# A second MLP whose residual is turned by DVE and ScalarE, with its norm's factor in the split inputs

## The chip, the cores and the metric

The kernel runs on one core of a Trainium2 chip. The metric is the device time of one execution in microseconds, as the median over several runs. Five engines work beside each other, each through its own queue in order: PE (matrix products, TensorE), DVE (VectorE), ACT (ScalarE), POOL (GpSimd) and SP (SyncE, which issues most DMAs). PEld is PE's loading of weights, which overlaps PE.

## The reference

A decoder trunk of two layers over 512 tokens of 1024 channels, in float32. Layer 0 mixes tokens by causal pooling, layer 1 by sliding-window attention; each mixer is followed by a gated MLP with a causal convolution of width 3 over the tokens. The change lies in the MLP of layer 1 and in the norm ahead of it:

```python
def rms_norm(x, g):
    xf = x.astype(jnp.float32)
    y = xf * lax.rsqrt(jnp.mean(xf * xf, axis=-1, keepdims=True) + RMS_EPS)
    return (y * g.astype(jnp.float32)).astype(x.dtype)

def conv_glu_ffn(h, w_in, conv_w, conv_b, w_out):
    u = h @ w_in
    c = lax.conv_general_dilated(
        u, conv_w[:, None, :].astype(u.dtype), window_strides=(1,),
        padding=[(CONV_W - 1, 0)], dimension_numbers=('NWC', 'WIO', 'NWC'),
        feature_group_count=2 * D_FF) + conv_b
    a, g = c[..., :D_FF], c[..., D_FF:]
    return (a * jax.nn.silu(g)) @ w_out
...
        hn = rms_norm(h, norm_ffn[i])
        h = h + conv_glu_ffn(hn, ffn_w_in[i], ffn_conv_w[i], ffn_conv_b[i], ffn_w_out[i])
    return rms_norm(h, norm_f)
```

D_FF is 2816. The factor of the norm, one number for each token, is the same for all channels of that token, so it may be applied to the inputs of the product with `w_in` or to its outputs.

## The kernel before

The residual `h` lies transposed: eight tiles `h[0]` to `h[7]` of 128 channels x 512 tokens, two to a buffer (`hp[0]` to `hp[3]`). Products are made from three passes: both operands are split into a high half (`_h`, rounded for PE) and a low half (`_l`, the rest), and `mm3` (L87) adds high x high (L89), high weight x low input (L90) and low weight x high input (L91). ScalarE makes the high half of a weight (L103) and DVE the low one (L106); `fetch` (L95) is SP's DMA. There are three buffers for raw weights and four for each half.

The attention stage ends with the output projection (L1229 to L1234). For each of eight `m` it adds PE's result to `h[m]` (DVE, L1232), splits `h[m]` times the norm's gain into `f1x{m}_h` (ScalarE, L243) and `f1x{m}_l` (DVE, L244), and gives the square (ScalarE, L211) to `norm2.add`, which adds it up on POOL (L220). These split inputs have the gain in them, but not the factor of the token.

The MLP of layer 1 (`mlp`, L770) runs `mlp_in` (L689). It has 44 chunks, (j, 1) and (j, 0) for j = 0 to 21: the gate and the value half of 128 columns. Chunks 0 to 3 are one group, with four PSUM banks side by side: for each of eight k, PE makes the three passes for all four. From chunk 4 on a group is one chunk, and six banks take turns. After the first group the program names the norm's sum (`norm.stats`, L222: a reduction on DVE at L225, a PE product over partitions at L226, and three Newton steps on DVE), after the second its spreading over the tokens (`norm.spread`, L231: ScalarE L234, DVE transpose L236), and then the convolutions of the chunks done so far.

`conv_chunk` (L678) multiplies the bank by the token factor `rb` into the SBUF tile `u` (L681), makes the first tap on ScalarE (L684) and adds the others on DVE (L685, L686). The gate half goes through Silu (L724), the two are multiplied (L733), and the products are summed and split (`split_sum`, L754) for the token stage. After each group `next(turns)` makes one step of `turned` (L785): four PE transposes of the residual (L792) into a bank and a ScalarE copy (L793) into `ht`, which has the tokens on its partitions; eight steps in all. `mlp_tokens` (L796) then adds the second product of the MLP to `ht`, in three sections, the first after chunk 17. It fetches its weights (L810, L811, L817) into the buffers of `hp` as those become free.

What runs when is set by a list scheduler at compile time: each engine's queue takes, of what is ready by the scheduler's own reckoning, what stands earliest in the source. `pin` (`keep_in_program_order`) chains an instruction behind the one traced before it on its engine; `issue_after(x)` queues the instructions of a block that are on `x`'s engine behind `x`. Neither makes an engine wait for anything by itself.

## Time and profile before

| | |
|---|---|
| median of 3 runs | 898.57 us (898.31 to 899.18) |
| the profiled execution | 897.72 us, of which span 895.9 us |
| second MLP's first matmul | 535.0 us after the span's start |
| granted TensorE clock, mean | 0.996 |
| DVE, ScalarE, POOL busy | 78%, 53%, 28% of the span |

The busy times in 40 equal slices of the span (22.4 us each), in tenths, with the clock that PE was granted:

```profile
PE   9999999999999999999999999999999999999996
PEld 8888889999999998898888888888888888888885
DVE  7899998878787876665887472999977888967744
ACT  7756655555464643546887451754534443434434
POOL 4867332313122300427665030001230002300004
PEclk9999999999999999999999999999999999999998
```

Times inside the execution are counted from the span's start. Where rows of the trace overlap (a matmul of 0.39 us starts 0.23 us after the one before), the distance between starts is what the engine needs for one, and the duration is what passes from its start to its result.

### The profile page before, as it was taken

Reading aid. Unit: us, or ns where it says so; the run is one execution under the profiler, and the core shown is the slowest. Engines: PE = TensorE matmul, PEld = TensorE weight load, DVE = VectorE, ACT = ScalarE, POOL = GpSimd, SP = SyncE. Lnnn points to the kernel's source line nnn. Section 1 sums busy time; section 2 is a strip of 40 time slices with the busy share of each in tenths; the row PEclk is TensorE's granted clock in tenths of the full one; section 3 lists DMA queues with packets and bytes.
Section 4 is the critical chain, followed back from the end, with each engine's and each line's share of the span. In section 5 each row is a group of like instructions: output and inputs, shape, how many; then the busy total and the mean of one; then the engine's idle time right before and its main releaser. Section 6 shows DMA issues by size and latency. Waiting matters only on the chain.

```text
span 895.9 us, 12904 instructions
## 1 busy us (share of the span) xinstructions
PE 884.4 (99%) x4770; PEld 765.6 (85%) x4770; DVE 698.0 (78%) x1110; ACT 475.6 (53%) x776; POOL 247.6 (28%) x327
## 2 busy tenths in 40 slices
PE   9999999999999999999999999999999999999996
PEld 8888889999999998898888888888888888888885
DVE  7899998878787876665887472999977888967744
ACT  7756655555464643546887451754534443434434
POOL 4867332313122300427665030001230002300004
PEclk9999999999999999999999999999999999999998
DMA  9444255565656443122110041175384231452202
GB/s 332 140 131 131 93 162 151 150 186 141 165 142 162 122 129 83 60 94 94 48 48 25 24 159 54 71 235 140 72 243 156 96 98 42 94 188 94 94 24 94
DMA packets 37118, 106.82 MB, mean 119 GB/s; under 512 B 3904, under 2 KB 5952, under 8 KB 37056
## 3 DMA queue, kind: packets, MB, share of 16 engines
q1 hardware_dynamic: 33600, 93.69, 31.8%
q0 software_dynamic: 3312, 12.06, 7.8%
q8 instruction: 37, 0.61, 0.3%
q10 hardware_dynamic: 144, 0.26, 0.1%
q14 instruction: 25, 0.20, 0.1%
HBM read 103.90 MB, written 2.10 MB: 118 GB/s over the span
## 4 chain that ended last, share of the span: by engine, by line
PE 89%; DVE 8%; ACT 1%; issue 1%; POOL 0%; ACTq 0%; DVEq 0%
PE bank L89 28%; PE bank L90 28%; PE bank L91 28%; PE bank L1157 1%; PE bank L1185 1%; DVE bank L393 1%; PE bank L288 1%; DVE tl L412 1%; DVE uw_hold_l L468 1%; PE bank L255 1%; DVE a_t L374 1%; ACT sc L1173 0%; DVE a_t L359 0%; DVE ty L420 0%; DVE g_t L358 0%
## 5 line engine op out<-in xcount | busy, mean ns | idle before, releaser
L89 PE MATMUL bank<-f1x_h,wi_h 128*128 128x512 f32 x352 | 137.7, 391 | 0.0
L90 PE MATMUL bank<-f1x_l,wi_h 128*128 128x512 f32 x352 | 137.0, 389 | 0.0
L91 PE MATMUL bank<-f1x_h,wi_l 128*128 128x512 f32 x352 | 136.8, 390 | 0.0
L103 ACT ACTIVATE wi_h<-wi_raw 128x1024 fp32r<-128x1024 f32 x58 | 61.3, 1060 | 86.5 <-PE bank L90 67.3
L91 PEld LDWEIGHTS bank<-f1x_h,wi_l 128*128 128x128 f32 x352 | 66.1, 188 | 13.9
L89 PEld LDWEIGHTS bank<-f1x_h,wi_h 128*128 128x128 f32 x352 | 66.1, 188 | 13.5
L90 PEld LDWEIGHTS bank<-f1x_l,wi_h 128*128 128x128 f32 x352 | 66.1, 188 | 13.5
L106 DVE TENSOR_TENSOR wi_l<-wi_raw,wi_h 128x1024 fp32r<-128x1024 f32 x44 | 53.8, 1225 | 27.0 <-ACT wi_h L103 27.0
L485 POOL TENSOR_TENSOR uw_r_raw<-uw_r_raw,uw_u_raw 128x512 f32<-128x512 f32 x15 | 25.0, 1668 | 161.7 <-DVE uw_hold_l L468 149.0
L106 POOL TENSOR_TENSOR wi_l<-wi_raw,wi_h 128x256 fp32r<-128x256 f32 x56 | 54.0, 994 | 27.3 <-ACT wi_h L103 27.3
L91 PE MATMUL bank<-th,uw_hold_l 128*128 128x256 f32 x180 | 50.9, 283 | 0.0
L90 PE MATMUL bank<-tl,uw_hold_h 128*128 128x256 f32 x180 | 50.9, 283 | 0.0
L89 PE MATMUL bank<-th,uw_hold_h 128*128 128x256 f32 x180 | 50.8, 282 | 0.0
L681 DVE TENSOR_TENSOR c_u<-bank,n_rb 128x512 f32<-128x512 f32 x44 | 30.1, 688 | 22.2 <-PE bank L91 22.0
L220 POOL TENSOR_TENSOR n_acc<-n_acc,n_sq 128x512 f32<-128x512 f32 x14 | 20.4, 1457 | 90.8 <-ACT n_sq L211 90.7
L90 PE MATMUL bank<-f0x_l,wi_h 128*128 128x512 f32 x112 | 43.6, 389 | 0.0
L91 PE MATMUL bank<-f0x_h,wi_l 128*128 128x512 f32 x112 | 43.6, 389 | 0.0
L89 PE MATMUL bank<-f0x_h,wi_h 128*128 128x512 f32 x112 | 43.0, 390 | 0.0
L531 DVE TENSOR_TENSOR h<-bank,h 128x512 f32<-128x512 f32 x48 | 32.9, 686 | 11.8 <-PE bank L91 11.4
L467 ACT ACTIVATE uw_hold_h<-wo_raw 128x512 fp32r<-128x512 f32 (+1 forms) x48 | 28.4, 591 | 25.7 <-PE bank L90 18.8
L686 DVE SCALAR_TENSOR_TENSOR c_t<-c_u,vec,c_t 128x510 f32<-128x510 f32 x44 | 40.9, 932 | 1.2
L823 POOL TENSOR_TENSOR wt_a_raw<-wt_a_raw,wt_s_raw 128x1024 f32<-128x1024 f32 x4 | 11.3, 2835 | 102.5 <-DVE wt_a_l L106 102.5
(437 smaller groups left out, 2771.6 us busy)
## 6 DMA issues: line engine op xcount, KB each, us to landing
wi_raw<-w_in SPq DMA_DIRECT2D x58, 512.0 KB, 3.3
wo_raw<-w_down SPq DMA_DIRECT2D x32, 256.0 KB, 2.7
uw_u_raw<-w_half SPq DMA_DIRECT2D x15, 512.0 KB, 5.5
uw_u_raw<-w_half POOLq DMA_DIRECT2D x15, 512.0 KB, 5.6
uw_r_raw<-w_half SPq DMA_DIRECT2D x15, 512.0 KB, 3.5
wt_a_raw<-w_tok SPq DMA_DIRECT2D x12, 512.0 KB, 3.8
kq_raw<-w_kq SPq DMA_DIRECT2D x10, 512.0 KB, 3.3
wo_raw<-w_o SPq DMA_DIRECT2D x8, 512.0 KB, 3.3
```

The source lines that it names most:

```text
L89: T.matmul(ps, lhsT=wh, rhs=xh, start=start, stop=False, **kw)
L90: T.matmul(ps, lhsT=wh, rhs=xl, start=False, stop=False, **kw)
L91: T.matmul(ps, lhsT=wl, rhs=xh, start=False, stop=stop, **kw)
L103: pin(A.activation(h[:, :n], raw[:, :n], AF.Copy))
L106: (eng or V).tensor_tensor(l[:, o], raw[:, o], h[:, o].bitcast(F32), ALU.subtract)
L220: eng.tensor_tensor(self.acc[:, lo:hi], self.acc[:, lo:hi], sq[:, lo:hi], ALU.add)
L467: A.activation(w[0], raw, AF.Copy)
L485: G.tensor_tensor(r[:, :n], r[:, :n], u[:, n:], ALU.add)
L531: V.tensor_tensor(h[m], ps, h[m], ALU.add)
L681: V.tensor_tensor(u, ps, rb, ALU.mult)
L686: V.scalar_tensor_tensor(t[:, 2:], u[:, : S - 2], cw[0], t[:, 2:], ALU.mult, ALU.add)
L823: G.tensor_tensor(r[:, :n], r[:, :n], raws["s1", s][:, :n], ALU.add)
```

## The change

The convolution no longer multiplies by the factor for chunks 4 to 43. For chunks 0 to 3 it does, now in place in the bank, and the taps of all chunks read the bank instead of the tile `u`, which is gone. The norm's sum is named inside the first group, before its third k, with ScalarE's square root in place of two of the Newton steps; the square root's table is loaded behind the fifth square of the attention stage, and the eighth square is added by DVE instead of POOL. Once the factor is there, the eight pairs `xs[k]` are made anew: `h[k]` times gain and factor (DVE), a high half by ScalarE and a low half by DVE, each written over the pair that the first group has read. The weights of chunk 4 are named between the fourth and the fifth of these, counted from 0, and those of chunks 5 and 6 behind the last. The convolutions of the first group queue behind all this.

`turned` makes four steps of a DVE transpose of `hp[e]` in blocks of 32 x 32, each followed by sixteen ScalarE copies that put a 32-partition piece (256 elements per partition) in its place in `ht`: 64 in all, 16 of them named in the first group, the rest as three behind each later convolution and one behind each Silu. The PE transposes are gone.

```diff
--- before.py
+++ after.py
@@ -95,6 +95,8 @@
         nc.sync.dma_start(raw[:, :n], src)
         return raw
 
+    lows = []
+
     def weights(src, n, name, eng=None, raw=None, step=1024, pin=lambda ins: ins):
 
         raw = raw or fetch(src, n, name)
@@ -103,7 +105,7 @@
         pin(A.activation(h[:, :n], raw[:, :n], AF.Copy))
         for a in range(0, n, step):
             o = slice(a, min(a + step, n))
-            (eng or V).tensor_tensor(l[:, o], raw[:, o], h[:, o].bitcast(F32), ALU.subtract)
+            lows.append((eng or V).tensor_tensor(l[:, o], raw[:, o], h[:, o].bitcast(F32), ALU.subtract))
         return h, l
 
     def part(w, k, m=P):
@@ -118,7 +120,7 @@
 
     def load_root(x, name):
 
-        A.activation(small(sm, 1, 32, tag="root", name=name), x, AF.Sqrt)
+        return A.activation(small(sm, 1, 32, tag="root", name=name), x, AF.Sqrt)
 
     load_root(eps, "root0")
 
@@ -208,7 +210,7 @@
 
         def square(self, c, lo, hi, sq=None):
             sq = sq or sm.tile([P, S], F32, tag="sq", name=f"{self.name}_sq{c}_{lo}")
-            A.activation(sq[:, lo:hi], h[c][:, lo:hi], AF.Square)
+            self.last = A.activation(sq[:, lo:hi], h[c][:, lo:hi], AF.Square)
             return sq
 
         def add(self, c, lo=0, hi=S, eng=G):
@@ -231,7 +233,7 @@
         def spread(self, r):
 
             wide = sm.tile([P, S], F32, tag="sq", name=f"{self.name}_wide")
-            A.activation(wide.rearrange("p (b i) -> p b i", i=SQ), r.unsqueeze(2).to_broadcast([P, NB, SQ]), AF.Copy)
+            self.wide = A.activation(wide.rearrange("p (b i) -> p b i", i=SQ), r.unsqueeze(2).to_broadcast([P, NB, SQ]), AF.Copy)
             rb = sm.tile([P, S], F32, tag="rb", name=f"{self.name}_rb", bufs=1)
             V.transpose(rb, wide)
             return rb
@@ -675,53 +677,79 @@
         for x in fills:
             pass
 
+    taps = []
+
     def conv_chunk(fp, layer, ps, rb, m, name):
 
-        u = fp.tile([P, S], F32, tag="u", name=f"{name}_u", bufs=3)
-        V.tensor_tensor(u, ps, rb, ALU.mult)
+        if rb is not None:
+            V.tensor_tensor(ps, ps, rb, ALU.mult)
         cw = [col(V_CW + (layer * 3 + t) * 2 * NF + m) for t in range(3)]
         t = fp.tile([P, S], F32, tag="t", name=f"{name}_t", bufs=4)
-        A.activation(t, u, AF.Identity, bias=col(V_CB + layer * 2 * NF + m), scale=cw[2])
-        V.scalar_tensor_tensor(t[:, 1:], u[:, : S - 1], cw[1], t[:, 1:], ALU.mult, ALU.add)
-        V.scalar_tensor_tensor(t[:, 2:], u[:, : S - 2], cw[0], t[:, 2:], ALU.mult, ALU.add)
+        taps.append(A.activation(t, ps, AF.Identity, bias=col(V_CB + layer * 2 * NF + m), scale=cw[2]))
+        V.scalar_tensor_tensor(t[:, 1:], ps[:, : S - 1], cw[1], t[:, 1:], ALU.mult, ALU.add)
+        taps.append(V.scalar_tensor_tensor(t[:, 2:], ps[:, : S - 2], cw[0], t[:, 2:], ALU.mult, ALU.add))
         return t
 
-    def mlp_in(fp, layer, xs, norm, ws0, z, turns):
+    def mlp_in(fp, layer, xs, norm, z, turns):
 
         pairs = [k for n, k in GROUPS for _ in range(n)]
         todo = [(j, s) for j in range(NF) for s in (1, 0)]
-        together = 4 if ws0 is None else 2
-        groups = [todo[i : i + together] for i in range(0, 4, together)] + [[t] for t in todo[4:]]
-        conv, pend, r, rb, y = [None, None], [], None, None, None
-        def load(group):
-            return [ws0.pop(0) if ws0 else in_weights(layer, j, s) for j, s in group]
+        groups = [todo[:4]] + [[t] for t in todo[4:]]
+        conv = [None, None]
+
+        def load(group, *more):
+            return [in_weights(layer, j, s, None, None, *more) for j, s in group]
+
+        def turn(n, *behind):
+            with ExitStack() as order:
+                for x in behind:
+                    order.enter_context(tc.issue_after(x.ins))
+                for x in range(n):
+                    next(turns, None)
+
+        def rescale(k):
+            y = fp.tile([P, S], F32, tag="t", name=f"xs{layer}_{k}", bufs=4)
+            V.scalar_tensor_tensor(y, h[k], col(V_NFF + layer * NC + k), rb, ALU.mult, ALU.mult)
+            return pin(A.activation(xs[k][0], y, AF.Copy)), V.tensor_tensor(xs[k][1], y, xs[k][0].bitcast(F32), ALU.subtract)
 
         stops, first = set(), 0
         for n, sums in GROUPS:
             first += 2 * n
             stops.add(min(first - 1 + sums, NF - 1))
-        ahead = load(groups[0])
+        ahead = [load(groups[0])]
         for i, group in enumerate(groups):
-            ws, ahead = ahead or load(group), None
+            ws = ahead.pop(0) if ahead else load(group)
             pss = [bank("ps") for j, s in group]
             for k in range(NC):
+                if i == 0 and k == 2:
+                    r = norm.stats(bank("aux"), root=True)
+                    turn(12, norm.last)
+                    rb = norm.spread(r)
+                    turn(4, norm.wide)
                 for w, ps in zip(ws, pss):
                     mm3(ps, part(w, k), xs[k], k == 0, k == NC - 1)
-            pend += zip(group, pss)
+            if i == 0:
+                for k in range(NC):
+                    if k == 5:
+                        ahead.append(load(groups[1], pin))
+                    behind = rescale(k)
+                for x in (2, 3):
+                    ahead.append(load(groups[x]))
+                    behind += (lows[-1],)
             j, s = group[-1]
-            if s == 1 or j not in stops:
-                ahead = load(groups[i + 1])
-            if rb is None:
-                if len(pend) < 4:
-                    continue
-                if r is None:
-                    r = norm.stats(bank("aux"))
-                    continue
-                rb = norm.spread(r)
-            for (j, s), ps in pend:
-                conv[s] = conv_chunk(fp, layer, ps, rb, s * NF + j, f"c{layer}_{j}_{s}")
+            if i and not ahead and (s == 1 or j not in stops):
+                ahead.append(load(groups[i + 1]))
+            for n, ((j, s), ps) in enumerate(zip(group, pss)):
+                with ExitStack() as order:
+                    for x in () if i else behind[: 3 + n // 2]:
+                        order.enter_context(tc.issue_after(x.ins))
+                    conv[s] = conv_chunk(fp, layer, ps, None if i else rb, s * NF + j, f"c{layer}_{j}_{s}")
+                if i:
+                    turn(3, *taps[-2:])
                 if s == 1:
-                    A.activation(conv[1], conv[1], AF.Silu)
+                    silu = A.activation(conv[1], conv[1], AF.Silu)
+                    if i:
+                        turn(1, silu, taps[-1])
                     continue
                 e, odd = divmod(j, 2)
                 if not odd:
@@ -746,10 +774,7 @@
                         split_sum(y, z[e], 2, 1, 6)
                 else:
                     split_sum(y, z[e], 2 * odd, 2 * odd, 2)
-                if s == 0:
-                    yield j
-            pend = []
-            next(turns, None)
+                yield j
 
     def split_sum(y, z, i, o, n, sign=1.0):
         src = y[:, i : i + n, :].rearrange("p a b -> p (a b)")
@@ -770,13 +795,16 @@
     def mlp(fp, xs, norm):
 
         z, ht = [], []
-        up = mlp_in(fp, 1, xs, norm, None, z, turned(fp, ht))
+        turns = turned(fp, ht)
+        up = mlp_in(fp, 1, xs, norm, z, turns)
         done, first = 0, 0
         for g, (n, sums) in enumerate(GROUPS):
             upto = first + 2 * n
             while done < min(upto + sums, NF):
                 done = next(up) + 1
             zg = z[first // 2 : upto // 2]
+            for x in turns:
+                pass
             if sums:
                 mlp_tokens(g, zg, ht)
             first = upto
@@ -784,14 +812,22 @@
 
     def turned(fp, ht):
 
-        for j in range(NT):
-            ht.append(fp.tile([P, D], F32, tag="ht", name=f"ht{j}", bufs=NT))
-            for a in range(2):
-                ps = bank("aux")
-                for c in range(4):
-                    T.transpose(ps[:, c * P : (c + 1) * P], h[4 * a + c][:, j * P : (j + 1) * P], ident)
-                A.activation(ht[j][:, a * S : (a + 1) * S], ps, AF.Copy)
-                yield
+        whole = fp.tile([P, NT, NC, P], F32, name="ht", bufs=1)
+        ht.extend(whole[:, j].rearrange("p c i -> p (c i)") for j in range(NT))
+        G4 = P // SQ
+        for e in range(NC // 2):
+            x = fp.tile([P, 2 * S], F32, tag="turn", name=f"turn{e}", bufs=1)
+            V.transpose(x, hp[e])
+            x = x.rearrange("p (c j q i) -> p c j q i", c=2, j=NT, q=G4)
+            for g in range(G4):
+                for q in range(G4):
+                    src, dst = slice(g * SQ, (g + 1) * SQ), slice(q * SQ, (q + 1) * SQ)
+                    A.activation(
+                        whole[dst, :, 2 * e : 2 * e + 2, src].rearrange("p j c i -> p c j i"),
+                        x[src, :, :, q, :],
+                        AF.Copy,
+                    )
+                    yield
 
     def mlp_tokens(g, z, ht):
 
@@ -1231,7 +1267,9 @@
                 pass
             V.tensor_tensor(h[m], wo_ps[m], h[m], ALU.add)
             xs2.append(split_scaled(h[m], col(V_NFF + NC + m), f"f1x{m}"))
-            norm2.add(m)
+            norm2.add(m, eng=V if m == NC - 1 else G)
+            if m == NC // 2:
+                pin(load_root(eps, "root2"))
 
 
     with tc.tile_pool(name="fp1", bufs=2) as fp:
```

## The prediction

> **What bounds the kernel now.** I began with the page's busy times and its chain that ended last, for the whole span.
>
> ```profile
> span 895.9 us, 12904 instructions
> ...
> PE 884.4 (99%) x4770; PEld 765.6 (85%) x4770; DVE 698.0 (78%) x1110; ACT 475.6 (53%) x776; POOL 247.6 (28%) x327
> ...
> PE 89%; DVE 8%; ACT 1%; issue 1%; POOL 0%; ACTq 0%; DVEq 0%
> ```
>
> PE is busy for 99% of the span and carries 89% of the chain. The next view is the chain for 530 to 620 us, where the second MLP starts and every edited line runs.
>
> ```profile
> by line: PE bank L91 32.2%; PE bank L90 32.1%; PE bank L89 31.9%; PE bank L792 3.9%; PE bank L226 0.1%
> ...
> 568.52 0.44 PE bank L792 x4
> ...
> 569.43 0.24 PE bank L91
> ```
>
> The whole stretch is PE: matmuls on L89 to L91, a trace of L226 (the norm's sum), and L792 at 3.9%: four transposes of the residual in one row of 0.44 us. The timeline of PE shows whether there is air between the matmuls.
>
> ```profile
> 535.00 0.39 PE L89 MATMUL bank<-f1x_h,wi_h 128*128 128x512 f32 x1
> ...
> 556.76 0.29 PE L226 MATMUL bank<-n_part,groups 128*128 128x16 f32 x2
> 556.90 0.48 PE L89 MATMUL bank<-f1x_h,wi_h 128*128 128x512 f32 x1
> ```
>
> From the first row to L226 the first group's 96 matmuls start in 21.76 us, 0.2267 us each, and the next group follows 0.14 us later: PE has no idle time. A chunk of eight k-steps with three matmuls each is 24 x 0.2267 = 5.44 us. So only two things change the time here: fewer PE instructions, or a new wait of PE.
>
> **The change, part by part.** The transposes go from PE.
>
> ```profile
> L792 PE MATMUL bank<-ident,h x32: 270/272/273, 562.4 to 604.2; 128*128 128x128 f32 x32
> ...
> L793 ACT ACTIVATE ht<-bank x8: 577/581/599, 563.5 to 604.8; 128x512 f32<-128x512 f32 x8
> ```
>
> There are 32, in eight blocks of four. The chain prices a block at 0.44 us: 8 x 0.44 = 3.5 us, and 3.9% of 90 us gives the same. A few matmuls behind each block take 0.24 us (569.43) for 0.23, so 0.3 us more over eight blocks is the most I grant: 3.8. I take 3.5. It lies wholly on the path. With the transposes go eight ScalarE copies of 0.58 us, 4.7 us, which no one waited for.
>
> What replaces them: four block transposes on DVE of 128x1024, each bounded by one and two times L236's 0.71 us below, and 64 ScalarE copies of 256 elements on 32 partitions. These and all later costs lie beside PE; they cost time only where PE gets an operand late. How much room there is:
>
> ```profile
> 537.00:555.00 18.00, 18.00 (x81) 14.85 (x81) 1.67 (x3) 0.48 (x2) 1.79 (x1) 1.00 0.14 48
> 557.00:606.00 49.00, 49.00 (x233) 40.48 (x233) 47.34 (x76) 31.85 (x43) 0.90 (x1) 1.00 0.49 153
> ```
>
> From 537 to 555 us DVE and ScalarE hardly work (1.7 and 0.5 us busy), while PE does the first group. From 557 to 606 us DVE is full (47.3 of 49 us) and ScalarE is not (31.9).
>
> **The norm, moved ahead.** Its sum (L226) stood at 556.8 us; it now stands before k-step 2 of the first group, at 535.0 + 24 x 0.2267 = 540.4 us. Its two PE instructions are moved, not removed. Are its inputs there? The last square ends at 537.2 us, and now DVE adds it instead of POOL:
>
> ```profile
> 536.55 0.62 ACT L211 ACTIVATE n_sq<-h 128x512 f32<-128x512 f32 x1
> ...
> 539.13 0.71 DVE L225 TRANSPOSE_TENSOR_REDUCE n_part<-n_acc 128x16 f32<-128x512 f32 x1 [1.18 <-POOL n_acc L220]
> ```
>
> DVE had idled 1.18 us before the reduction (L225), so it is free at 538.0; one add like L681 (0.69) and the reduction (0.71) end at about 539.4, a microsecond before PE asks. If a block transpose (up to 1.4 us) slips in ahead, PE waits 0.4 us; I cost it at 0 and keep 0.4. From the sum to the spread factor I take layer 0, which uses the square root already:
>
> ```profile
> L226 PE MATMUL bank<-n_part,groups x6: 177/220/263, 44.2 to 556.8; 128*128 128x16 f32 x6
> ...
> L236 DVE STREAM_TRANSPOSE n_rb<-n_wide x3: 705/711/711, 47.9 to 562.6; 128x512 f32<-128x512 f32 x3
> ```
>
> First sum 44.2, end of its transpose 47.9 + 0.7 = 48.6: 4.4 us, with other work among it. So the factor stands at about 545 us, against 563.3 before. One more ScalarE table load, for the root, stands behind the fifth square, near 524 us:
>
> ```profile
> 529.53 1.06 ACT L103 ACTIVATE wi_h<-wi_raw 128x1024 fp32r<-128x1024 f32 x1 [3.24 <-PE bank L90]
> ...
> 554.69 2.96 ACT L103 ACTIVATE wi_h<-wi_raw 128x1024 fp32r<-128x1024 f32 x3 [17.52 <-PE bank L90]
> ...
> 567.29 1.28 ACT L724 ACT_TABLE_LOAD   x1 [0.99 <-DVE c_t L686]
> ```
>
> It takes 1.28 us, and ScalarE idled 3.24 us before 529.53 with only PE's buffer to wait for: nothing. (The load at 567.29, for Silu, stays.)
>
> **The inputs, split anew.** The durations:
>
> ```profile
> L685 DVE SCALAR_TENSOR_TENSOR c_t<-c_u,vec,c_t x44: 742/745/752, 565.1 to 856.8; 128x511 f32<-128x511 f32 x44
> ...
> L106 DVE TENSOR_TENSOR wi_l<-wi_raw,wi_h 128x1024 fp32r<-128x1024 f32 x26 | 31.8, 1226 | 21.6 <-ACT wi_h L103 21.6
> L681 DVE TENSOR_TENSOR c_u<-bank,n_rb 128x512 f32<-128x512 f32 x22 | 14.9, 687 | 5.3 <-PE bank L91 5.1
> L759 DVE TENSOR_TENSOR zl<-y,zh 128x1536 fp32r<-128x1536 f32 x5 | 8.8, 1756 | 0.2 <-ACT zh L757 0.2
> L761 DVE SCALAR_TENSOR_TENSOR zl<-y,zh 128x256 fp32r<-128x256 f32 x5 | 2.1, 420 | 0.5 <-ACT zh L757 0.5
> ...
> L684 ACT ACTIVATE c_t<-c_u,vec 128x512 f32<-128x512 f32 x22 | 17.5, 806 | 1.5 <-DVE c_u L681 1.3
> L757 ACT ACTIVATE zh<-y 128x256 fp32r<-128x256 f32 x5 | 2.0, 409 | 3.9 <-DVE y L733 3.9
> L234 ACT ACTIVATE n_wide<-n_r 128x512 f32<-128x512 f32 x1 | 0.6, 631 | 0.2 <-DVE n_r L200 0.2
> ```
>
> Eight times a product (0.75, like L685), a ScalarE copy (at most 0.63) and a difference (0.69): 8 x 1.44 = 11.5 us of DVE, from 545 to 556.5, inside its idle stretch. Each pair is written in place, so pair 7 waits for the first group's last read at 557.0. ScalarE's copies 1 to 7 are chained to the one before, and 5 to 7 stand behind chunk 4's high half, which waits for PE's buffer (554.69, 1.06 us): free from 555.8, so not in the way. Pair 7 comes at 557.0 + 0.63 + 0.69 = 558.3, and with one weight split (1.23) queued ahead of it at 559.6. PE wants pair 7 after 21 more matmuls, at 556.9 + 4.8 = 561.7. Two microseconds are left: cost 0.
>
> **The convolutions.** Forty chunks lose L681 (0.69), the first four keep it. The taps now read PSUM. L685 above reads SBUF; layer 0's tap reads PSUM:
>
> ```profile
> L358 DVE SCALAR_TENSOR_TENSOR g_t<-bank,vec,g_t x22: 732/750/751, 52.9 to 336.7; 128x511 f32<-128x511 f32 x22
> ```
>
> From PSUM 0.750, from SBUF 0.745 us: I take no difference, and 1.4 us less DVE work for each pair of chunks.
>
> The Trainium skill speaks against this part: its page "VectorE: DVE Perf Modes", section "Rules for kernel authors", has a matmul's output copied to SBUF first where several operations use it, and the section "The TRN2 errata" there gives PSUM sources 62 cycles more. As an estimate from that page this would be 0.06 us a tap, 0.8 us over the twelve taps ahead of chunk 7 below, and rival A would be that much dearer. The two rows do not bear it out.
>
> **Weights of three chunks named ahead.** What PE needs next are the low halves of chunk 7 and 8 (chunks counted from 0). Before:
>
> ```profile
> 555.78 2.36 DVE L106 TENSOR_TENSOR wi_l<-wi_raw,wi_h 128x1024 fp32r<-128x1024 f32 x2 [15.94 <-ACT wi_h L103]
> ...
> 561.47 1.23 DVE L106 TENSOR_TENSOR wi_l<-wi_raw,wi_h 128x1024 fp32r<-128x1024 f32 x1
> ...
> 582.09 1.22 DVE L106 TENSOR_TENSOR wi_l<-wi_raw,wi_h 128x1024 fp32r<-128x1024 f32 x1
> ...
> 562.52 1.06 ACT L103 ACTIVATE wi_h<-wi_raw 128x1024 fp32r<-128x1024 f32 x1 [0.25 <-DMA wi_raw<-w_in]
> ```
>
> The first row is chunks 4 and 5, chunk 6 follows at 558.15, then 7 and 8. Chunk 8's high half was ready at 563.6 and its low one came 18.5 us later: DVE worked off convolutions that stand earlier in the source. Now chunk 7 is the one named after them. DVE from 555.8 until chunk 7's low half, if it goes strictly by the source: three low halves 3.7, three differences 2.1, four convolutions 4 x (0.69 + 0.75 + 0.75) = 8.8, two gate products 1.4, the pair's sums and splits 0.42 + 0.69 + 0.42 + 0.42 + 1.76 = 3.7, chunks 4 and 5 3.0 and 1.1, one block transpose 1.4: 25.2 us, to 581.0; 26 starts each some 0.09 us before the former's end (562.61 less 561.47 is 1.14, not 1.23) make it 578.7, and the half 579.9. PE reaches chunk 7 at 556.9 + 3 x 5.44 = 573.2. It can do its 16 matmuls on the high half first, to 576.8, and chunk 8's, to 580.5. That PE's order does such things the chain shows:
>
> ```profile
> 580.37 0.44 PE bank L792 x4
> 580.81 0.23 PE bank L89
> ...
> 583.07 0.44 PE bank L792 x4
> 583.50 0.36 PE bank L91
> ```
>
> No L91 between 580.4 and 583.5: while the low half was out, PE did high halves and four blocks of transposes. I take 0, since DVE also meets gaps of the Silu chain; the other end is 579.9 - 576.8 = 3.1 us.
>
> **SP's and POOL's queues.** The token stage's weights are fetched into the residual's four buffers as they come free.
>
> ```profile
> SPq L817 <- PE bank L792: 23.2, 2, 20.5
> ...
> 604.70 0.42 SPq L810 DMA_DIRECT2D wt_s_raw<-w_tok  x1
> ...
> wt_s_raw<-w_tok POOLq DMA_DIRECT2D x8, 512.0 KB, 7.4
> ```
>
> Before, such a fetch stood 20.5 us at the head of SP's queue for the transposes, and the last buffers came free with the last block. Now a buffer is free with its block transpose: the first by 545 us, the fourth at the 33rd step after the first group's 16, seven steps to a pair, so behind chunk 13, which PE ends at 556.9 + 10 x 5.44 = 611.3. Its fetch (604.7 before) goes out near 614, and with about 5 us for SP's part and 7.4 for POOL's adding one it lands by 627. The stage's first matmul comes after chunk 17, at 633. Cost 0, with 6 us in hand; chunk weights queued behind a waiting fetch have three buffers ahead of them.
>
> Sum: -3.5 on PE, +0 elsewhere, ends -3.8 and +3.5 of waits (0.4 + 3.1). The profiled execution took 897.72 us (span 895.9, 1.8 around it) and would take 894.2; the three runs' median is 0.85 above it, so 898.57 - 3.5 = 895.1.
>
> **The rivals.**
> A, the cover is gone (18%): the transposes were what PE did while a low half was late. Then their four blocks come back as a wait, 1.8 us, or chunk 7's 3.1: 896.8 to 898.2. For it: DVE's 47.3 of 49 us. Against: eight L681 (5.5 us) leave that stretch, and the rescaling lies before it.
> B, the rescaled inputs come late (12%), slower: the chain sum, root, spread, eight rescalings is serial and PE cannot pass chunk 4 without it. It decides from a factor later than 561.7 - 11.5 = 550.2 us. Should the sum keep its old place in PE's queue, the factor stands at 563.3 as before, pair 7 at 574.8, and PE waits 13.1: 908.2. A factor at 556 costs 5.8 and gives 900.9. Against: by the rows above the factor stands 5 us before 550.2.
> C, ScalarE becomes the bound (4%), slower: a pair of chunks lasts 10.9 us and takes ScalarE 2 x 1.06 + 2 x 0.81 + 0.63 (Silu, the size of L234) + 1.0 (splits: half of L757's 0.41 and 1.5 x 1.06) = 5.4 plus seven copies, so it decides from 0.79 us a copy; at 1.0 us seven pairs run 1.5 over each, 10.3: 905.4. The bounds, 0.41 (L757) and 0.63 (L234, twice the elements), stay under; I take 0.41. The Trainium skill's section "The TRN2 errata" (same page) warns of this: small pieces each pay a fixed cost, and it advises 512 elements or more. Its formula gives, as an estimate, 0.40 us for 256 elements, and L757's 0.41 agrees.
>
> **How the numbers follow.** Forecast 66%, A 18, B 12, C 4. A third of A still ends over 0.2% (1.8 us, about what a measurement of this kernel can tell) below 898.57: faster 0.66 + 0.06 = 0.72, same 0.12, slower 0.12 + 0.04 = 0.16. The range reaches from the largest saving (894.8) to A's end (898.2), with the 0.6 us by which a run shown lies off the median on both sides: 894.2 to 898.8, leaving out B and C and the far end of the waits.
>
> **What would show it.** Right: no L792, PE without idle from 535 us, the span shorter by 3.5; L226 near 540.4, the factor by 546, pair 7's difference before 561; DVE's busy time down by 10 us or more (40 x 0.69 less 11.5 and 5.6). Wrong: PE waiting for xs's pair or for L106's low half between 557 and 585 us, or starts further apart than 0.2267 us; copies over 0.79 us.

## The result and the profile after

| | before | after |
|---|---|---|
| median of the runs shown with the result | 898.88 us (898.28 to 899.78, 6 runs) | 893.17 us (893.01 to 894.47, 6 runs) |
| profiled execution | 897.72 us, span 895.9 | 893.14 us, span 891.3 |

The ratio is 0.994, interval 0.9927 to 0.9953; a second measurement of the kernel after gave 0.9942 (0.9930 to 0.9955), which is 5.2 us (4.0 to 6.3) of 899.01. The forecast was 3.5 us, to 895.1, with a range down to 894.2. So the sign was right, and the time lies 1 us below the range. The page's first lines and its chain of waits, for the kernel after:

```profile
span 891.3 us, 12896 instructions
...
PE 881.1 (99%) x4738; PEld 763.0 (86%) x4738; DVE 682.6 (77%) x1083; ACT 502.8 (56%) x843; POOL 242.7 (27%) x326
...
PE 88%; DVE 8%; ACT 2%; issue 1%; POOL 0%; ACTq 0%; DVEq 0%
```

PE has 32 instructions and 3.3 us less, and 99% of the span as before. The chain for 535 to 625 us, which held 3.9% of transposes, is now only matmuls:

```profile
by line: PE bank L91 33.5%; PE bank L89 33.4%; PE bank L90 33.3%; PE bank L228 0.1%
```

Does PE wait? All its waits in the whole span (the releasing engine and line, total us, times, longest):

```profile
PE bank L257 <- DVE warm L255: 2.2, 1, 2.2
PE bank L89 <- DVE h L533: 0.7, 1, 0.7
```

The first is at the program's start, the second at 118 us, far ahead of the second MLP; within that MLP there is none. So the new work hides entirely, as forecast. What the MLP saved is read from PE's timeline, between its first matmul and the first of the token stage (columns: start, duration, engine, line, operation, output<-inputs, shapes):

```profile
535.58 0.39 PE L89 MATMUL bank<-f1x_h,wi_h 128*128 128x512 f32 x1
...
541.08 0.29 PE L228 MATMUL bank<-n_part,groups 128*128 128x16 f32 x2
...
633.82 0.39 PE L89 MATMUL bank<-wt_a_h,zh 128*128 128x512 f32 x1
```

```profile
637.02 0.39 PE L89 MATMUL bank<-wt_a_h,zh 128*128 128x512 f32 x1
```

Before, that stretch ran from 535.00 (quoted in the prediction) to 637.02: 102.02 us. After, 633.82 - 535.58 = 98.24. The saving is 3.78 us, the upper end of the 3.5 to 3.8 that the transposes were given. I call this stretch the **MLP part** below. From there to the last matmul both kernels take 250.01 us.

But the spans differ by 4.6 us, and the first stretch even grew by 0.58. The rest is at the very end. ScalarE's timeline for the last microseconds, before and after:

```profile
890.73 2.36 ACTq L941 DMA_DIRECT2D out<-o  x1
```

```profile
887.54 0.37 ACTq L977 DMA_DIRECT2D out<-o  x1
```

The same DMA, issued from the same place in the program, holds ScalarE's queue for 2.36 us before and for 0.37 after. From the last matmul's start to the span's end it is 895.89 - 887.03 = 8.86 us before and 891.31 - 883.83 = 7.48 after: 1.38 us that no step of the prediction had. The DMA view of that window of the kernel before names a companion (queue, kind: packets, MB, share):

```profile
q14 instruction: 1, 0.01, 0.5%
...
out<-o ACTq DMA_DIRECT2D x1, 256.0 KB, 4.0
```

One packet on a queue of the kind "instruction" moves there, and the output lands 4.0 us after its issue. In the kernel after, the corresponding window has no such packet, and the landing takes 2.6 us:

```profile
out<-o ACTq DMA_DIRECT2D x1, 256.0 KB, 2.6
```

3.78 + 1.38 - 0.58 = 4.58, the difference of the spans. The questions for the experiments: is the end's 1.4 us real and what makes it; are the 3.8 us the transposes alone; and what do the other parts of the change do, if PE shows no trace of them? One of the eight executions behind the median of "after, not named ahead" in the table below took 1792.4 us, for no known reason, and the ratio there leaves it out.

### The profile page after: what moved, and what is told of

It reads as the page before. It is cut to its first block, busy times and chain, and to the rows that moved or that the text cites. A ratio compares the mean times of both kernels' runs of the same rounds, so it can differ in the third digit from the quotient of the medians.

```text
span 891.3 us, 12896 instructions
## 1 busy us (share of the span) xinstructions
PE 881.1 (99%) x4738; PEld 763.0 (86%) x4738; DVE 682.6 (77%) x1083; ACT 502.8 (56%) x843; POOL 242.7 (27%) x326
## 3 DMA queue, kind: packets, MB, share of 16 engines
q1 hardware_dynamic: 33600, 93.69, 31.9%
## 4 chain that ended last, share of the span: by engine, by line
PE 88%; DVE 8%; ACT 2%; issue 1%; POOL 0%; ACTq 0%; DVEq 0%
PE bank L89 28%; PE bank L90 28%; PE bank L91 28%; PE bank L1193 1%; PE bank L1221 1%; DVE bank L395 1%; PE bank L290 1%; DVE tl L414 1%; ACT sc L1209 1%; PE bank L257 1%; DVE uw_hold_l L470 1%; DVE a_t L376 1%; DVE a_t L361 0%; DVE g_t L360 0%; DVE ty L422 0%
## 5 line engine op out<-in xcount | busy, mean ns | idle before, releaser
L89 PE MATMUL bank<-f1x_h,wi_h 128*128 128x512 f32 x352 | 137.0, 389 | 0.0
L90 PE MATMUL bank<-f1x_l,wi_h 128*128 128x512 f32 x352 | 136.9, 389 | 0.0
L105 ACT ACTIVATE wi_h<-wi_raw 128x1024 fp32r<-128x1024 f32 x58 | 61.4, 1059 | 59.5 <-PE bank L90 43.8
L90 PEld LDWEIGHTS bank<-f1x_l,wi_h 128*128 128x128 f32 x352 | 66.1, 188 | 13.7
L89 PEld LDWEIGHTS bank<-f1x_h,wi_h 128*128 128x128 f32 x352 | 66.1, 188 | 13.5
L90 PE MATMUL bank<-tl,uw_hold_h 128*128 128x256 f32 x180 | 50.9, 283 | 0.0
L89 PE MATMUL bank<-th,uw_hold_h 128*128 128x256 f32 x180 | 50.8, 282 | 0.0
L90 PE MATMUL bank<-f0x_l,wi_h 128*128 128x512 f32 x112 | 43.6, 389 | 0.0
L89 PE MATMUL bank<-f0x_h,wi_h 128*128 128x512 f32 x112 | 43.0, 390 | 0.0
L847 POOL DMA_DIRECT2D wt_s_raw<-w_tok x8 | 7.0, 870 | 120.1 <-DMA wt_s_raw<-w_tok 72.7
L470 DVE TENSOR_TENSOR uw_hold_l<-wo_raw,uw_hold_h 128x512 fp32r<-128x512 f32 (+1 forms) x48 | 36.7, 764 | 3.2 <-ACT uw_hold_h L469 3.2
L1209 ACT ACTIVATE sc<-sc,neg 128x257 f32<-128x257 f32 (+1 forms) x64 | 30.3, 476 | 10.6 <-DVE neg L1196 10.0
```

The costliest lines, as they stand in the source:

```text
L89: T.matmul(ps, lhsT=wh, rhs=xh, start=start, stop=False, **kw)
L90: T.matmul(ps, lhsT=wh, rhs=xl, start=False, stop=False, **kw)
L105: pin(A.activation(h[:, :n], raw[:, :n], AF.Copy))
L470: V.tensor_tensor(w[1], raw, w[0].bitcast(F32), ALU.subtract)
L1209: A.activation(t, t, AF.Exp, bias=neg[:, i : i + 1], scale=-1.0, accum_out=den[:, i : i + 1])
```

## The experiments

Ten more runs were made, one of them of the kernel after once more. The table has for each the MLP part, the time from the last matmul's start to the span's end (both from its one trace), the median and the ratio to the kernel before, measured beside it. Medians of different rows were not all taken beside the same runs of before, so the ratios compare better.

| kernel | MLP part, us | end, us | median, us | ratio (interval) |
|---|---|---|---|---|
| before | 102.02 | 8.86 | 898.88 | 1 |
| after | 98.24 | 7.48 | 893.17 | 0.994 (0.9927 to 0.9953) |
| after again | 98.27 | 7.47 | 893.30 | 0.9942 (0.9930 to 0.9955) |
| before + 40 copies | 102.07 | 7.48 | 897.94 | 0.9985 (0.9976 to 0.9993) |
| after + 56 copies | 98.28 | 7.49 | 893.93 | 0.9944 (0.9924 to 0.9964) |
| after + 60 copies | 98.24 | 8.90 | 895.28 | 0.9956 (0.9941 to 0.9972) |
| after, PE transposes | 102.06 | 7.48 | 898.17 | 0.9982 (0.9973 to 0.9991) |
| after, late norm | 110.61 | 7.47 | 906.98 | 1.0082 (1.0069 to 1.0096) |
| after, not named ahead | 106.09 | 7.46 | 901.48 | 1.0027 (1.0017 to 1.0038) |
| after, factor behind | 103.85 | 7.48 | 899.97 | 1.0014 (1.0004 to 1.0024) |
| before, turn only | 106.47 | 7.49 | 902.08 | 1.0033 (1.0020 to 1.0045) |
| before, turn held | 108.15 | 7.48 | 903.96 | 1.0059 (1.0044 to 1.0075) |

### The end: before with 40 small copies

```diff
-                if s == 0:
-                    yield j
+                if j == 15:
+                    for x in range(40):
+                        pin(A.activation(small(sm, 1, 32, tag="root", name=f"pad{x}"), eps, AF.Copy))
+                yield j
```

> The kernel before, with 40 extra ScalarE copies of 32 elements on one partition issued at chunk 15's group of the second MLP, where the low halves lead PE by over 10 us; nothing else differs. Theory F: the kernel before loses about 1.4 us at its very end because ScalarE's issue of the last output DMA took 2.36 us in its trace, while one 8 KB packet of instructions was fetched on its queue; the kernel after issues it in 0.37 us because its ScalarE program has other lengths. Moving ScalarE's instruction count by 40 then takes the slow issue away: issue of the last DMA 0.3 to 0.5 us, time from the last matmul to the span's end 8.9 -> 7.5 us, time 1.2 to 2.0 us below the kernel before's (about 0.998 of it). Rival: the long issue comes from something else (the output's data, the chip's memory, chance), or it is part of the change itself: issue still near 2.4 us in this profile, time within 0.5 us of the kernel before (ratio 1.000).

The last DMA's issue on ScalarE's timeline:

```profile
893.03 0.37 ACTq L943 DMA_DIRECT2D out<-o  x1
```

0.37 us, the end 7.48, the median 1.6 us and the ratio's middle 1.3 us (0.6 to 2.2) below the kernel before. Forty instructions that do nothing, the last of them 120 us earlier (772 us), made the kernel before faster. Theory F holds in this direction; the rival (chance, or a part of the change) falls.

### The end: after with 56 and 60 small copies

The same loop in the kernel after, with 56 and with 60.

> The kernel after with 56 extra tiny ScalarE copies at chunk 15's group. Theory F (ScalarE's last DMA issue is long when an 8 KB fetch of instructions on its queue falls beside it; fetches stand 128 instructions apart): the fetch moves toward the last DMA's issue, and in one of the three kernels with 56, 60 and 64 copies it falls on it: issue 2.36 us in place of 0.37 and the time from the last matmul to the end 7.5 -> 8.9 us. With 56: the nearest by the count, likeliest with 60. MLP part unchanged at 98.2. Rival: 7.5 us in all three.

> The kernel after with 60 extra tiny ScalarE copies at chunk 15's group. Theory F: as for 56 copies; by the count of ScalarE's instructions this one puts the boundary of a fetch nearest to the last DMA's issue: issue 2.36 us, last matmul to the end 8.9 us, time about 1.4 us above after's (894.6). Rival: 7.5 us as in after.

The last DMA with 56 copies, and then with 60, with the instruction packet in the last microseconds of the latter:

```profile
888.96 0.37 ACTq L980 DMA_DIRECT2D out<-o  x1
```

```profile
888.54 2.39 ACTq L980 DMA_DIRECT2D out<-o  x1
```

```profile
q14 instruction: 1, 0.01, 0.9%
```

With 56 copies nothing happens; with 60 the slow issue is back (2.39 us), the packet of instructions is back beside it, and the end is 8.90 us. Both kernels have the same MLP part. The ratios (0.9944 and 0.9956, from two and four executions) differ by 1.1 us, within their intervals; the traces show the 1.4 directly. A kernel with 64 copies was not run.

That the packet fetches ScalarE's own instructions can be counted in the traces, where ScalarE's instructions (those of its sequencer included) can be numbered. An 8 KB packet of this kind starts right behind the 1088th in the kernel before and right behind the 1216th, 128 further on, with 60 copies; the output's DMA is the 1088th and the 1216th, and is being issued at that moment. With 40 copies the DMA is the 1127th, and the packet goes behind the 1085th, at 856.6 us, 36 us ahead of the DMA. With 56 the DMA is the 1212th, and the packet comes at 893.2 us, after the span's end. In the kernel after the DMA is the 1157th. (Single records can be missing, so the numbers may be off by one or two.)

So the number of instructions on ScalarE's queue decides whether a fetch of its next instructions falls on its last DMA, and 1.4 us of this change's result is that. It belongs to no edited line, and an edit that changes the number of ScalarE's instructions can win or lose it. What the fetch and the issue share was not taken apart; shown is that they come and go together.

### The transposes: after with PE's transposes put back

```diff
-                    turn(12, norm.last)
...
-                    turn(4, norm.wide)
...
-                    turn(3, *taps[-2:])
+                    next(turns, None)
...
-                    if i:
-                        turn(1, silu, taps[-1])
...
+                    for x in range(56):
+                        pin(A.activation(small(sm, 1, 32, tag="root", name=f"pad{x}"), eps, AF.Copy))
...
+                    T.transpose(ps[:, c * P : (c + 1) * P], h[4 * a + c][:, j * P : (j + 1) * P], ident)
+                A.activation(ht[j][:, a * S : (a + 1) * S], ps, AF.Copy)
```

> The kernel after, with the residual turned by 32 PE transposes and 8 ScalarE copies of 512 elements as before, one block per chunk from chunk 4 on, and 56 tiny ScalarE copies at chunk 15 in place of the missing ones, so that ScalarE's instruction count stays that of after. Theory: the transposes alone are what the MLP part saves, so they come back in full: 3.5 to 3.8 us above after's time (896.7 to 897.0), eight rows of 0.44 us in the chain of waits, no other idle time of PE. Rival (rival A of the prediction): PE had idle time or late low halves that transposes cover, or after wins by its other parts too: then less than 2 us above after's time (under 895.2).

The chain of waits for 535 to 625 us, by line:

```profile
by line: PE bank L89 32.3%; PE bank L90 32.1%; PE bank L91 31.9%; PE bank L819 3.9%; PE bank L228 0.1%
```

The 3.9% are back, and the MLP part is 102.06 us: 3.82 more than after, 0.04 from the kernel before. The ratio's middle is 0.0040 above that of after, 3.6 us. The transposes are the whole of what the MLP part saved, 0.48 us for a block: 0.44 for the four, and the rest from the first matmuls behind each, which start 0.24 us apart.

### Rival B's price: after with the norm's sum behind the first group

```diff
                 if i == 0 and k == 2:
-                    r = norm.stats(bank("aux"), root=True)
                     turn(12, norm.last)
-                    rb = norm.spread(r)
-                    turn(4, norm.wide)
...
             if i == 0:
+                r = norm.stats(bank("aux"), root=True)
+                rb = norm.spread(r)
+                turn(4, norm.wide)
```

> The kernel after with the norm's sum and spread issued behind the first group's matmuls instead of ahead of its third k-step; everything else as in after. This prices rival B of the prediction. Theory: the chain from sum to pair 7's difference is serial and PE cannot pass chunk 4 without it: the sum at about 557 us, the factor at 561 to 563, pair 7 near 573 to 575, and PE idle for 10.8 to 13.1 us between 557 and 575, so 904 to 906.3 us. Rival: PE covers part of it by working k-steps in the order in which the pairs come and by other work: idle under 6 us, time under 899.2.

PE's timeline where it waits (in brackets the idle time ahead of the instruction, and what ended it):

```profile
568.57 0.80 PE L89 MATMUL bank<-f1x_h,wi_h 128*128 128x512 f32 x1 [9.68 <-ACT wi_h L105]
569.16 0.63 PE L90 MATMUL bank<-f1x_l,wi_h 128*128 128x512 f32 x1
```

The MLP part is 12.4 us longer, the theory's 10.8 to 13.1; the rival's cover of 5 us or more is not there. But it is made otherwise than I worked it out: PE stands still for 9.7 us, and then its matmuls start 0.43 us apart, not 0.23, up to 573.1. That second piece is 2.4 us. So PE went on from 568.6 us, at half rate, while the last pairs were still being made, and that the sum comes out near the forecast is in part luck. The profile names a high half (L105) as what came last for the 9.7 us, and ScalarE's timeline shows why:

```profile
566.28 1.29 ACT L713 ACTIVATE f1x_h<-xs 128x512 fp32r<-128x512 f32 x2 [1.84 <-DVE xs L712]
567.48 1.04 ACT L105 ACTIVATE wi_h<-wi_raw 128x1024 fp32r<-128x1024 f32 x1
```

Chunk 4's high half is named between pairs 4 and 5, so it stands behind the copies of the first five pairs, and these wait for DVE. PE waited for the place of chunk 4's weights in that order, not for pair 7.

### The weights ahead: after without naming them

```diff
-                for x in (2, 3):
-                    ahead.append(load(groups[x]))
-                    behind += (lows[-1],)
```

> The kernel after without naming the weights of the third and fourth group (chunks 5 and 6 of the order) ahead of the first group's convolutions; each is named one group ahead, as in the kernel before. Theory: the low halves of chunks 5 to 7 stand behind four or more convolutions on DVE then; by after's trace chunk 5's and 6's halves led PE by 3.3 and 7.0 us and chunk 7's by 3.7, and four convolutions (4 x 2.2 = 8.8 us) ahead of them use that up: PE waits 1.8 to 5.5 us on L91's operand, MLP part 100.0 to 103.7 us against 98.2. Rival: PE goes on with high halves of the next chunk and the naming is worth nothing: 98.2 to 98.6.

PE's timeline:

```profile
569.89 0.39 PE L90 MATMUL bank<-f1x_l,wi_h 128*128 128x512 f32 x1
575.30 0.80 PE L91 MATMUL bank<-f1x_h,wi_l 128*128 128x512 f32 x1 [5.02 <-DVE wi_l L108]
```

The last six matmuls up to 569.89 are L89 and L90 alone, so PE used a high half while its low one was out, but for no more than these six; then it stands for 5.0 us. The wait is within the theory's 1.8 to 5.5, but the MLP part is 7.85 us longer, since the next twelve matmuls run 0.43 us apart (2.6 us in all). Removing three lines costs more than the whole change brings.

### The rescaled inputs: after with the factor on every chunk

```diff
-                for k in range(NC):
-                    if k == 5:
-                        ahead.append(load(groups[1], pin))
-                    behind = rescale(k)
+                ahead.append(load(groups[1], pin))
+                behind = ()
...
-                    for x in () if i else behind[: 3 + n // 2]:
+                    for x in () if i else behind[: 1 + n // 2]:
...
-                    conv[s] = conv_chunk(fp, layer, ps, None if i else rb, s * NF + j, f"c{layer}_{j}_{s}")
+                    conv[s] = conv_chunk(fp, layer, ps, rb, s * NF + j, f"c{layer}_{j}_{s}")
```

> The kernel after without the rescaled inputs: the norm's sum and factor stay early, but every chunk's product is multiplied by the factor in its bank (44 products of 0.69 us on DVE in place of 4), and the eight rescalings (8 x 1.44 us of DVE in its idle stretch) are left out. Theory: DVE's work between 557 and 606 us grows by 8 chunks x 0.69 = 5.5 us and it had 47 of 49 us: with the turn's steps in it, low halves of chunks 8 and 9 (0.8 and 0.4 us ahead of PE in after) come late and PE waits 0.5 to 5 us: MLP part 98.8 to 103.2. Rival: the products hide beside PE as they did before, the rescaling is worth nothing and its saving of DVE work is idle time: 98.2 to 98.6, and the last chunks run no later.

PE's timeline at its wait within the MLP part:

```profile
581.07 0.50 PE L91 MATMUL bank<-f1x_h,wi_l 128*128 128x512 f32 x1 [3.66 <-DVE wi_l L108]
```

3.7 us for one low half, and 5.6 us on the MLP part with the slow matmuls behind it: more than the theory's 5. DVE's timeline has the half late:

```profile
579.80 1.22 DVE L108 TENSOR_TENSOR wi_l<-wi_raw,wi_h 128x1024 fp32r<-128x1024 f32 x1
```

DVE does not pause between 570 us and that row, and each chunk's product takes it 0.69 us. A second wait, of 0.53 us, comes in the token stage (at 652.87), and the stretch from the token stage's first matmul to the last one is 0.8 us longer than in after. The rival (hidden anyway, the last chunks no later) falls.

### The turn alone: before with only the block transposes

```diff
-        u = fp.tile([P, S], F32, tag="u", name=f"{name}_u", bufs=3)
+        u = ps
         V.tensor_tensor(u, ps, rb, ALU.mult)
...
-            next(turns, None)
+            for x in range(5):
+                next(turns, None)
```

with the new function that turns the residual.

> The kernel before with only the turn of the residual by DVE and ScalarE (five steps behind each group); the norm, the scale on each chunk and the weights named one chunk ahead stay as they were (the factor is multiplied in the bank in place, since the separate tile would not fit beside the turned residual). Theory: the other parts of the change pay only for DVE's time; without them the four block transposes (1.24 us each) and the 44 products come on top of DVE's queue where it is full, chunk 7's and 8's low halves come later than PE wants them, and PE waits: 1.8 to 3.1 us of the 3.8 saved are given back in the MLP part, first MLP matmul to first token matmul 100.0 to 101.3 us against 102.0 before and 98.2 after. Rival: the transposes' saving stands by itself, and the moved norm, the rescaled inputs and the weights named ahead are worth nothing: 98.2 to 98.6 us, as after.

It is slower than before, 106.47 us for the MLP part. PE waits four times there, for 0.95, 3.06, 0.58 and 1.08 us. The longest wait, on ScalarE's timeline and on PE's:

```profile
554.21 6.81 ACT L798 ACTIVATE ht<-turn 32x256 f32<-32x256 f32 x16 [1.31 <-DVE turn L793]
561.04 2.95 ACT L103 ACTIVATE wi_h<-wi_raw 128x1024 fp32r<-128x1024 f32 x3
```

```profile
562.15 0.50 PE L89 MATMUL bank<-f1x_h,wi_h 128*128 128x512 f32 x1 [3.06 <-ACT wi_h L103]
```

Three lots of sixteen copies, from 537.94 us on, stood ahead of the next chunks' high halves on ScalarE (the expectation below counts 42 of them, the trace has 48). The direction was the theory's, the mechanism at this place was not: ScalarE's order, not DVE's load. The three short waits the profile does put down to DVE. So a second kernel holds the steps, as the change does:

```diff
+                if layer and i == 0 and k == 2:
+                    turn(16, norm.last)
...
+                if layer:
+                    turn(4, *taps)
```

> The kernel before with only the turn by DVE and ScalarE, and the steps held as in the kernel after: 16 of the 68 behind the norm's last square, where DVE and ScalarE idle, and four behind each chunk's last tap. Without the hold (the run before this one of that kind) ScalarE took 42 of the copies ahead of the high halves of chunks 4 to 6, and PE waited 3.1 us for them. Theory S: that run lost its time to the copies' place in ScalarE's queue; held, the turn by itself saves most of the transposes' 3.8 us: MLP part 98.2 to 99.5 us. Rival D: DVE is the limit there without the rescaled inputs and the weights named ahead; PE waits for low halves all the same, with the clock at half rate behind the wait: MLP part 101 to 106 us, as in the runs that leave out one of those two parts (103.9 and 106.1).

PE's timeline, at the longer of its two waits (the other is 0.95 us):

```profile
595.05 0.79 PE L91 MATMUL bank<-f1x_h,wi_l 128*128 128x512 f32 x1 [6.85 <-DVE wi_l L106]
```

Theory S's number falls: with no copies ahead of the high halves of chunks 4 to 6 the MLP part is 108.15 us, longer still than the 101 to 106 of rival D. One low half comes 6.9 us late. On DVE's timeline it stands (at 593.78) behind a tap that waits for ScalarE:

```profile
593.11 0.75 DVE L687 SCALAR_TENSOR_TENSOR c_t<-bank,vec,c_t 128x511 f32<-128x511 f32 x1 [1.21 <-ACT c_t L686]
```

ScalarE's timeline has eight copies ahead of the first tap that this one waits for:

```profile
588.88 3.40 ACT L809 ACTIVATE ht<-turn 32x256 f32<-32x256 f32 x8
592.30 0.78 ACT L686 ACTIVATE c_t<-bank,vec 128x512 f32<-128x512 f32 x1
```

So the copies' place in ScalarE's queue still mattered, now ahead of the taps, and S's idea is not refuted with its number. How much of the 6.9 us is theirs was not taken apart, and both kernels also multiply in the bank in place, where the kernel before has a tile of its own, for want of room. What they do show is that the turn by itself, in these two orders, loses 4.5 and 6.1 us in the MLP part against the kernel before.

### After again

> The kernel after, unchanged, timed in more rounds. The two differences that the traces show are 3.8 us in the second MLP (the transposes) and 1.4 us in ScalarE's last DMA issue: 5.2 us, so a ratio of 0.9942 and about 893.5 to 894.3 us. The first result's 5.7 us would then hold 0.5 us of the run-to-run spread that lies in the first 112 us of every kernel here. Rival: a third gain of the change is still unnamed and the ratio is 0.9936 or less.

The median is 893.30 us and the ratio 0.9942, the theory's value; 0.9936 lies within the interval too, so a further gain below half a microsecond cannot be excluded. The runs fall at 893.2 to 893.3 and at 894.4 to 894.5, and this trace shows one source of such steps: its second MLP starts at 536.91 us, 1.33 later than in the first trace of the same kernel. Over the traces of all kernels here, which differ little up to that point, the start lies between 535.00 and 537.45. Three places make it, all in the first 120 us. In the chain of waits, the 24 warming matmuls at the start take 4.72 us in the trace of before and 5.41 in this one (5.39 in the first trace of after):

```profile
2.23 4.72 PE bank L255 x24
```

```profile
2.23 5.41 PE bank L257 x24
```

Near 110 us PE waits for ScalarE in some traces and not in others. The first trace of after has no such wait; its timeline in this one:

```profile
111.34 0.39 PE L89 MATMUL bank<-th,uw_u_h 128*128 128x256 f32 x1 [0.59 <-ACT sn L650]
```

And the wait for DVE at 118 to 120 us is 0.66 us in the first trace of after and 0.97 in this one. Between these two traces the last two places make nearly all of the difference. The profiled execution of before had the earliest start of all, 0.85 us below its median as a whole. This spread is what a single pair of profiles adds to any comparison here.

## Where the prediction was right, and the step that failed

**PE's transposes.** Right, and under-sized. The block of 0.44 us was measured as 0.48 with what follows it (3.82 us over eight, in the run that puts them back). I had granted 3.8 and taken 3.5; the rows of 0.24 us behind each block were already evidence for the larger value. That is 0.3 us.

**"+0 elsewhere".** This is the step that failed. The sum let ScalarE's eight copies go and 64 come at no cost because no one waits for them, which is right, and took the rest of the program to be untouched, without a reason given. But a step that adds or removes instructions on ScalarE also shifts the places at which its later instructions are fetched (128 apart in these traces), and in the kernel before one of these sat on the last thing that ScalarE does, its 1088th instruction. Its row was there to be read: 2.36 us for a DMA issue, the landing at 4.0 us, and one packet of kind "instruction" in that window. I had followed the chain in the stretch of the edits and had not looked at the 9 us behind the last matmul. It gave 1.4 us, shown by the padded kernels in both directions.

**The range.** Its low end was the largest saving, 3.8, plus 0.6 us of spread. With the end's 1.4 us the sum is 5.2, and 898.57 - 5.2 = 893.4, below it. The second measurement gives these 5.2 us; the half microsecond more in the first (5.7) is within the spread described above and has no cause shown.

**The norm moved ahead.** L228 stands at 541.08, forecast 540.4 plus the 0.58 by which this trace starts later. Its inputs came later than I said, on DVE's timeline:

```profile
536.39 1.24 DVE L820 STREAM_TRANSPOSE turn<-h 128x1024 f32<-128x1024 f32 x1
...
538.77 1.22 DVE L108 TENSOR_TENSOR wi_l<-wi_raw,wi_h 128x1024 fp32r<-128x1024 f32 x1
539.91 0.71 DVE L227 TRANSPOSE_TENSOR_REDUCE n_part<-n_acc 128x16 f32<-128x512 f32 x1
...
544.88 0.71 DVE L238 STREAM_TRANSPOSE n_rb<-n_wide 128x512 f32<-128x512 f32 x1 [0.76 <-ACT n_wide L236]
...
560.14 0.68 DVE L713 TENSOR_TENSOR f1x_l<-xs,f1x_h 128x512 fp32r<-128x512 f32 x1
```

A block transpose slipped in ahead (the case I had kept 0.4 us for), and a low half besides: the reduction ends at 540.62, not 539.4. That left 0.4 us of margin, and PE lost 0.05. The root then stood behind twelve copies on ScalarE:

```profile
537.72 5.11 ACT L825 ACTIVATE ht<-turn 32x256 f32<-32x256 f32 x12
542.85 0.27 ACT L184 ACTIVATE rs_y<-bank,eps 128x16 f32<-128x16 f32 x1
```

It starts 1.5 us after the sum's end at 541.37. Even so the factor stands at 545.6, against 545 to 546 forecast: luck in part, since the 4.4 us taken over from layer 0 happened to leave room for a wait of 1.5 us that I had not seen.

**The rescaling.** Products 0.75, differences 0.68 as priced; pair 7's difference ends at 560.8, 1.2 us after my later bound of 559.6 (0.58 of it is the later start) and before PE's need (561.7, with the later start 562.3). Cost 0, with 1.5 us left. The late-norm run gives the price if that order is lost, 12.4 us; I had said 13.1 for the old place, all of it a wait for pair 7, and 2.4 of the 12.4 are the clock, not a wait.

**Taps, turn and copies.** The rows that group them, for 530 to 625 us (columns: shapes, count, busy us, mean ns):

```profile
L825 ACT ACTIVATE ht<-turn 32x256 f32<-32x256 f32 x55 | 22.8, 415 | 3.5 <-DVE turn L820 2.8
...
L689 DVE SCALAR_TENSOR_TENSOR c_t<-bank,vec,c_t 128x511 f32<-128x511 f32 x15 | 11.1, 744 | 1.6 <-ACT c_t L688 1.6
```

Taps from the bank take 0.744 us, where SBUF gave 0.746: the Trainium skill's page "VectorE: DVE Perf Modes", section "The TRN2 errata", with its 62 cycles more for PSUM is not borne out by this kernel for a tap whose other input lies in SBUF. The 0.415 us of a copy agrees with the 0.40 that the formula in the same section of the Trainium skill gave as an estimate, and is far from the 0.79 at which rival C would decide. The block transpose is 1.24 us (L820 above), within the bounds of 0.71 and 1.4.

**Low halves.** Taken as 0, with 3.1 us as the far end: 0 was right. Windows of 537 to 555 and 557 to 606 us (columns: length, then PE, weight loads, DVE, ScalarE and POOL busy with counts, then clock, DMA share, GB/s):

```profile
537.00:555.00 18.00, 18.00 (x82) 14.81 (x81) 13.59 (x24) 11.32 (x25) 0.00 (x0) 1.00 0.25 86
557.00:606.00 49.00, 49.00 (x218) 40.52 (x217) 46.10 (x62) 40.97 (x66) 0.90 (x1) 1.00 0.50 151
```

Most of the rescaling and a quarter of the turn's copies (16 of 64) did go into the idle stretch (DVE from 1.7 to 13.6 us, ScalarE from 0.5 to 11.3), and in the full stretch DVE went from 47.3 to 46.1 us only, and ScalarE from 31.9 to 41.0. So **rival A** was close at hand rather than wrong: it did not happen, but each of the three runs that take out one of the parts beside the turn makes PE wait, by 5.6 to 12.4 us on the MLP part. I had costed those parts at 0 and left it there; the better reading is that they are worth nothing by themselves (with PE's transposes put back the MLP part was that of before) and that, in the orders tried here, the 3.8 us were not to be had without them. The far end of 3.1 us was also too small: it counted on sixteen matmuls that PE would do on a high half, and then the next chunk's, while the low one is out. In each trace with such a late half (those with waits of 5.0, 3.7 and 6.9 us, and the kernel before, from 580.56 us) PE did six, and then stood or, in the kernel before, did transposes. With six the far end is 579.9 - 574.6 = 5.3 us.

**Queues.** PE's waits show none for the token stage's weights: 0, as taken.

## What to carry to other kernels

Where one engine has no gaps, taking instructions off it is worth their full time, including the slower starts behind them; the work that replaces them is free only if its order is arranged, and each supporting edit is judged by taking it out of the finished kernel, not by what it shows in the profile. Read the whole chain to its last instruction before making the sum: an operation whose row is several times longer than its like is a cost that any edit, even an idle one, can move. When two profiles are compared, split the span at a few instructions that both have, so that a late start and a short end are not booked on the edit.

## What the runs showed of the hardware

A packet of ScalarE's instructions beside a DMA issue of ScalarE made that issue 2.4 us long, not 0.37, and the output's landing 4.0 us, not 2.6. The packets stand 128 of ScalarE's instructions apart; the others in the kernels before and after lay beside no DMA issue of ScalarE, which has just the one, and left no wait of PE in the second MLP.

After a wait of 3 us or more, PE's 512-column matmuls start 0.427 us apart instead of 0.227, for 3 to 5 us. It followed each of the long waits here (3.1, 3.7, 5.0, 6.9 and 9.7 us) and none of the waits of 0.95 and 1.08 us in the two runs with the turn only, and it added 1.6 to 2.6 us. The granted clock shows it, here in the run with the factor behind, around its wait from 577.4 to 581.07 us and after it (the clock is the third figure from the end):

```profile
577.40:582.00 4.60, 0.94 (x5) 0.80 (x5) 4.58 (x6) 3.17 (x9) 0.64 (x1) 1.00 0.41 114
582.20:585.50 3.30, 3.30 (x10) 2.52 (x9) 3.30 (x6) 2.02 (x4) 0.06 (x1) 0.50 0.62 173
```

The stretches at 0.5 in the five runs last 3.41 us or two or three times that. The Trainium skill's page "TensorE: Matmul & The Clock Gate", section "Part 1: The HAM clock gate (the "warmup" mystery)", gives 426.7 ns for a cold array at 512 columns, and the trace agrees. The same section of the Trainium skill names an idle window of about 3.4 us as what makes the array cold. Here less than a whole window of waiting was enough: in the runs with waits of 3.1 and 3.7 us the clock fell 1.4 and 1.1 us after these had ended, and of the 3.41 us before the fall PE had waited 2.6 (a second wait of 0.58 included) and 2.3. So a late operand costs more than the wait that the profile names.

A tap that read SBUF took 2.77 us while POOL added two weight tiles (L823, 2.83 us from 623.08 on); four of the 44 taps of that line did so. On DVE's timeline of the kernel before:

```profile
623.69 2.77 DVE L686 SCALAR_TENSOR_TENSOR c_t<-c_u,vec,c_t 128x510 f32<-128x510 f32 x1
```

In the kernel after no tap exceeds 0.752 us, and two of them, which now read the bank, lie wholly beside such an add of POOL. The first, on DVE's and POOL's timelines:

```profile
745.61 0.75 DVE L690 SCALAR_TENSOR_TENSOR c_t<-bank,vec,c_t 128x510 f32<-128x510 f32 x1
```

```profile
745.00 2.40 POOL L859 TENSOR_TENSOR wt_a_raw<-wt_a_raw,wt_s_raw 128x1024 f32<-128x1024 f32 x1 [82.96 <-DVE wt_a_l L108]
```

So a tap from the bank was not lengthened where one from SBUF was. A weight split on DVE, which has both of its inputs in SBUF, took 2.76 us beside POOL's add of 2.40. In neither kernel did PE wait for any of these, so their cost on the path was not measured.
